# Four plain column tiles ahead of the seven-product sets in the first feed-forward, with the norm product, the first loads and the odd pool moved

## The chip, the cores and the metric

The kernel runs on one core of one Trainium2 chip. The metric is the device time of one execution in microseconds; the runs of the kernel before have a median of 1270.05 us (1269.68 to 1270.89, three runs). All names of lines (L463) are lines of the kernel before, unless a row comes from the changed kernel and says so.

## The reference

One block on x of shape 512 x 1024 in float32: a feed-forward with half weight, a mixer, a second feed-forward with half weight, and a final RMS norm.

```
x = x + 0.5 * swiglu(rmsnorm(x, g1), ffn1_w_gu, ffn1_w_down)     # D_FF = 2816
x = x + hybrid_mixer(rmsnorm(x, gm), w_in, ...)                  # conv + gated linear attention
x = x + 0.5 * swiglu(rmsnorm(x, g2), ffn2_w_gu, ffn2_w_down)
return rmsnorm(x, final_g)

swiglu(h, w_gu, w_down): g, u = split(h @ w_gu);  (silu(g) * u) @ w_down
```

The gate and the up half of `w_gu` are 2816 columns wide each, which is 22 column tiles of 128, and the reduction over 1024 is 8 k tiles.

## The kernel before

**Precision and weights.** x lies transposed in SBUF, 8 tiles `x[k]` of 128 features by 512 positions. Every float32 operand is split into a high and a low part (`wh`/`wl` for weights, `opA`, `opB` or `tp` pairs for data), and each product is three matmuls: wh by high, wh by low, wl by high. Weights arrive by DMA on SP's queue into `f` tiles (L248); ScalarE casts the high part (L273) and VectorE subtracts it for the low part (L274). `Weights.issue` does this, two units ahead of the matmuls, and `STEPS` holds the order of the units; the `f` ring has 10 tiles in the feed-forwards, `wh` and `wl` three each.

**First stage of a feed-forward.** `mm_group` (L325) multiplies the four column tiles 0 and 1 of gate and up, k by k, twelve matmuls of 512 columns for one k. Its data operands are x times the gain, not yet normed (`Norm.add`: L377 or L374 the high part, L378 the low part, L383/L386 the square, L387 the running sum `acc`). Behind the sixth k tile (`if k == 5`), `norm.finish` issues the product of `acc` with a matrix of ones (L407, L408) and the chain that makes 1/rms: transpose L410, small operations L411 to L434, copy L419, transpose L423. Its result `row` scales the group's results as they leave PSUM (L437).

**Sets.** The other 20 column tiles of each half go through ten sets of two tiles by a scheme of seven products in place of eight (m1, p2, q6, p5, q7, p4, p3). A product is 24 matmuls of 256 columns (L463), so a set has 168. The data operands of the products (`Operands.make`) are made once, from x normed with `row`: `normed` (L554, four instructions for a quarter), differences of quarters (L501 to L510), then a cast on ScalarE (L487) and a subtraction on VectorE (L488). A set's weights are four blocks of 512 KB; VectorE adds one sum (L261) and POOL's queue adds three by accumulating DMAs (L252). In the first feed-forward `xo.make("m1")` and `xo.make("p2")` come straight behind the group, then the two pairs of results are taken out of PSUM (times `row`, silu L568, product L437).

**The rest.** The down projection runs from `hid` (L301 to L303 with `opB` operands). The mixer's last three projections, w_out_conv, w_out_gla and w_o, have split `tp` tiles as data operands: 8, 8 and 4 column tiles by `mm_single` (L301 to L303, 24 matmuls each, 480 in all) and four by `mm_group` (L325, 96). The second feed-forward transposes X on TensorE in between (L645, L646).

**Order.** TensorE, VectorE, ScalarE and POOL run their streams in order, each in an order that the tile framework's scheduler chose from the program's text; SP's and POOL's queues issue DMAs in order too. At the start of the program the loop over k issues `x[k]`'s load and, for k of 0, 1, 2 and 4, `W.issue()`; the very first of these also loads the four blocks of the first set, because `loads` places a set's blocks six steps ahead of its first product.

**Places in SBUF.** Pools are stacked: `front`, `keep` (X), `wh`, `wl`, `opA`, `acc_row`, and then the pools of the phase. In the mixer these are `f` (4 tiles), the odd pool (`cpool`, small constants) and `tp` (50 tiles of 2048 bytes). In the built program of the kernel before, `opA` and `wh` tiles start 96 bytes behind a multiple of 2048, `opB` tiles 1120 bytes behind one, and the mixer's `tp` tiles 32 bytes behind one.

Of the kernel before, what the change touches and what calls it, by code (L numbers as in the profile page):

```python
# [15 lines left out]
P = 128  # L16
# [19 lines left out]
V_G1, V_GM, V_G2, V_GLA, V_CONV, V_GB = 0, 8, 16, 24, 32, 56  # L36
NVEC = 60
WARM = 10


def k_parts(kt):
# [53 lines left out]

PLAN = []
STEPS = []
ENDS = []  # L100
# [5 lines left out]
        PLAN.append(u)  # L106


def ffn_plan(up, down, slow):
    units(group(up, KD, (0, DFF, P, DFF + P), slow))  # L110
    firsts = []
    for s in range(1, KF // 2):
        firsts.append(len(PLAN))
        PLAN.extend((up, 4 * j, 4, (i * DFF + s * HW,), HW) for i in range(2) for j in range(2))
    STEPS.extend(order(firsts))
    units(full(down, KF))
    ENDS.append(len(STEPS))
# [23 lines left out]
    ENDS.append(len(STEPS))  # L141


ffn_plan("ffn1_w_gu", "ffn1_w_down", True)
mixer_plan()
ffn_plan("ffn2_w_gu", "ffn2_w_down", False)


def offset(n):
# [5 lines left out]
def block_kernel(ctx: ExitStack, tc: tile.TileContext, xT, vecs, gf, gup, wgl, wts, out):  # L155
# [236 lines left out]
    def rstd_rows(accs, width):  # L392


        n = len(accs)
        cnt[0] += 1
        i = cnt[0]

        def small(tag):
            t = acc_row.tile([P, HEADS * 16], F32, tag=tag, name=f"{tag}{i}")  # L400
            return t[:, : 16 * n]

        v, s, r, q = small("st_v"), small("st_s"), small("st_r"), small("st_q")
        for a, acc in enumerate(accs):
            h, l = split(acc)
            st = AUX()
            nc.tensor.matmul(st, ones_r, h, start=True, stop=False)  # L407
            nc.tensor.matmul(st, ones_r, l, start=False, stop=True)  # L408
            t = T()
            nc.vector.transpose(t, st)  # L410
            nc.vector.tensor_scalar(  # L411
                out=v[:, 16 * a : 16 * (a + 1)],
                in0=t.rearrange("p (b c) -> p b c", c=32)[:, :, 0],
                scalar1=1.0 / width, scalar2=EPS, op0=ALU.mult, op1=ALU.add)
        newton_rsqrt(r, v, s, q)
        rows = []
        for a in range(n):
            t = T()
            nc.vector.tensor_copy(  # L419
                t.rearrange("p (b c) -> p b c", c=32),  # L420
                r[:, 16 * a : 16 * (a + 1)].unsqueeze(2).to_broadcast([P, 16, 32]))
            row = acc_row.tile([P, S], F32, tag="row", name=f"row{i}") if n == 1 else T()
            nc.vector.transpose(row, t)  # L423
            rows.append(row)
        return rows
# [106 lines left out]
            sets[n].run(p)  # L532


    def ffn(up, down, norm, nxt):
        xh, xl = norm.h, norm.l
        rows = []

        def finish(k):
            if k == 5:  # L540
                rows.append(norm.finish())

        o = mm_group(up, KD, (0, DFF, P, DFF + P), xh, xl, extra=finish, slow=nxt is not None)
# [15 lines left out]
            return xn[j, l]  # L559

        xo = Operands(normed, 4)
        xo.make("m1")
        xo.make("p2")
        hid = [tile_of("hid", [P, 2, S])]
        for e in range(2):
            s, t = T(), T()
            mul(s, o[2 * e], row)
            nc.scalar.activation(s, s, AF.Silu)  # L568
            mul(t, o[2 * e + 1], row)
            mul(hid[0][:, e], s, t)  # L570

        def up_set(i):
            h = tile_of("hid", [P, 2, S])
# [74 lines left out]
    def last_down(us, split_hid):  # L648
# [72 lines left out]

        with tc.manual_schedule(engines={ENG.PE, ENG.DVE, ENG.Activation, ENG.Pool}):

            early = keep.tile([P, 1], F32, tag="early", name="early")
            nc.scalar.activation(early, hl[1][:, 1, 0:1].bitcast(F32), AF.Square)
            nc.scalar.activation(early, early, AF.Sqrt)
            for t in range(NTB):
                sm = keep.tile([P, 8], F32, tag="fin", name=f"fin{t}", bufs=2)
                fin.append([sm[:, i : i + 1] for i in range(6)])
                part(t, 0)  # L730
                if t > 0:
                    rstd(t - 1)
                    store(t - 1, 0)
                part(t, 1)
                if t > 0:
                    store(t - 1, 1)
            rstd(last)
            store(last, 1)
            store(last, 0)


    def mixer(norm, nxt):
# [16 lines left out]
        gl_raw = cpool.tile([P, KD, RANK], F32, tag="glraw", name="gl_raw")  # L759
        nc.sync.dma_start(gl_raw, wgl)  # L760
        gl_w = cpool.tile([P, KD, 3, 2 * RANK], F32R, tag="glw", name="gl_w")
        reset = T()
        nc.gpsimd.memset(reset, 1.0)
        nc.gpsimd.memset(reset.rearrange("p (c t) -> p c t", t=CH)[:, :, 0:1], 0.0)
# [299 lines left out]
    with phase("small1", **FFN):  # L1064
        W.phase(1)
        n1 = Norm(V_G1)
        for k in range(KD):
            nc.sync.dma_start(x[k], xT[k])
            if k < 2 or k % 2 == 0 and k < 6:
                W.issue()  # L1070
        W.early = 5
        for k in range(KD):
            n1.add(k, sooner=True)
        nm = Norm(V_GM)
        ffn("ffn1_w_gu", "ffn1_w_down", n1, nm)
    with phase("small2", f=4, small=1, tp=50):
        W.phase(2)
        n2 = Norm(V_G2)
        mixer(nm, n2)
    with phase("small3", **FFN):  # L1080
        W.phase(5)
        ffn("ffn2_w_gu", "ffn2_w_down", n2, None)


# [41 lines left out]
```

## Time and profile before

| | us |
|---|---|
| median of three runs | 1270.05 |
| the profiled execution | 1270.03 |
| its span (first to last instruction) | 1268.3 |
| TensorE busy in the span | 1231.4 |
| VectorE, ScalarE, POOL busy | 700.8, 502.4, 121.1 |
| mean granted TensorE clock | 0.987 of full speed |

What lies around the span is 1270.03 - 1268.3 = 1.7 us. A row of the timeline gives the start in us, the time to the end of its last instruction, engine, line, operation, output and inputs, the count, and in brackets the engine's idle time just before with what ended it. Matmuls overlap their neighbours, so the rate is read from the distance of starts, not from durations.

### The profile page before, as it was taken

What the parts mean: (1) busy time and instruction counts of PE and PEld (TensorE: products, weight loads), DVE (VectorE), ACT (ScalarE), POOL (GpSimd) and SP (SyncE); (2) the same over time, 40 slices, a digit from 0 to 9 for tenths busy, and PEclk for the clock granted to TensorE, in tenths of its full rate; (3) what the DMA queues carried; (4) which work ended last, traced back from release to release, by engine and by line L of the source; (5) the groups of instructions that cost most, each with busy time, mean ns of one, the idle gap of its engine ahead of it and who ended that gap; (6) DMA issues with size and microseconds to landing.
All of it is one profiled execution on the core that took longest, in us unless ns stands there. A gap on an engine that the chain in (4) does not pass through costs nothing.

```text
span 1268.3 us, 16985 instructions
## 1 busy us (share of the span) xinstructions
PE 1231.4 (97%) x7018; PEld 1081.6 (85%) x7018; DVE 700.8 (55%) x823; ACT 502.4 (40%) x640; POOL 121.1 (10%) x137
## 2 busy tenths in 40 slices
PE   8799999999999999999999999999889999999996
PEld 6699999988878788888888888888679999998885
DVE  6876666633365664453585334445676666663335
ACT  5454444522242542222334222323364444452233
POOL 1011111000010071000112000000011111100003
PEclk9799999999999999999999999999899999999999
DMA  8377777532013232222223333231558777763201
GB/s 299 84 181 195 182 182 187 173 115 67 36 53 120 87 97 83 67 84 83 83 83 100 100 100 90 94 100 34 189 131 198 185 187 175 187 181 98 67 1 67
DMA packets 43613, 152.91 MB, mean 121 GB/s; under 512 B 5040, under 2 KB 5168, under 8 KB 43536
## 3 DMA queue, kind: packets, MB, share of 16 engines
q1 hardware_dynamic: 34752, 120.34, 28.4%
q0 software_dynamic: 8640, 31.46, 14.1%
q8 instruction: 55, 0.90, 0.3%
q14 instruction: 22, 0.18, 0.0%
q10 hardware_dynamic: 144, 0.03, 0.0%
HBM read 118.26 MB, written 2.10 MB: 95 GB/s over the span
## 4 chain that ended last, share of the span: by engine, by line
PE 89%; DVE 4%; ACT 3%; issue 2%; DMA 2%; SPq 0%; POOL 0%; DVEq 0%; ACTq 0%
PE mm L463 29%; PE mm L302 13%; PE mm L301 13%; PE mm L303 13%; PE mm L325 5%; PE mm L662 2%; PE mm L661 2%; PE mm L660 2%; PE mm L343 1%; PE aux L302 1%; PE aux L303 1%; PE aux L301 1%; PE mm L344 1%; PE mm L342 1%; DVE wl L274 1%
## 5 line engine op out<-in xcount | busy, mean ns | idle before, releaser
L273 ACT CAST wh<-f 128x1024 fp32r<-128x1024 f32 (+1 forms) x281 | 293.5, 1046 | 614.7 <-PE mm L302 233.7
L274 DVE TENSOR_TENSOR wl<-f,wh 128x1024 fp32r<-128x1024 f32 (+1 forms) x281 | 344.8, 1229 | 269.1 <-ACT wh L273 267.1
L463 PE MATMUL mm<-opA,wh 128*128 128x256 f32 x1280 | 235.1, 284 | 3.5 <-ACT opA L487 2.8
L463 PEld LDWEIGHTS mm<-opA,wh 128*128 128x128 f32 x1280 | 200.8, 193 | 4.5 <-ACT opA L487 3.0
L463 PE MATMUL mm<-opB,wh 128*128 128x256 f32 x960 | 179.7, 287 | 7.7 <-ACT opB L487 6.7
L463 PE MATMUL mm<-opA,wl 128*128 128x256 f32 x640 | 181.8, 284 | 0.4 <-DVE wl L274 0.4
L301 PE MATMUL mm<-opA,wh 128*128 128x512 f32 x416 | 163.5, 393 | 0.0
L302 PE MATMUL mm<-opA,wh 128*128 128x512 f32 x416 | 162.9, 392 | 0.0
L303 PE MATMUL mm<-opA,wl 128*128 128x512 f32 x416 | 162.1, 390 | 0.0
L463 PEld LDWEIGHTS mm<-opB,wh 128*128 128x128 f32 x960 | 152.9, 195 | 9.0 <-ACT opB L487 7.6
L463 PE MATMUL mm<-opB,wl 128*128 128x256 f32 x480 | 137.3, 286 | 0.0
L463 PEld LDWEIGHTS mm<-opA,wl 128*128 128x128 f32 x640 | 123.3, 193 | 0.7 <-DVE wl L274 0.7
L252 POOL DMA_DIRECT2D f<-f x60 | 51.7, 861 | 628.4 <-DVE wl L274 294.6
L463 PEld LDWEIGHTS mm<-opB,wl 128*128 128x128 f32 x480 | 93.7, 195 | 0.0
L301 PEld LDWEIGHTS mm<-opA,wh 128*128 128x128 f32 x416 | 78.1, 188 | 16.4
L303 PEld LDWEIGHTS mm<-opA,wl 128*128 128x128 f32 x416 | 78.1, 188 | 16.1
L302 PEld LDWEIGHTS mm<-opA,wh 128*128 128x128 f32 x416 | 78.1, 188 | 16.1
L437 DVE TENSOR_TENSOR tp<-mm,tp 128x512 f32<-128x512 f32 x36 | 24.8, 691 | 105.8 <-PE mm L303 105.1
L303 PE MATMUL mm<-tp,wl 128*128 128x512 f32 x160 | 63.0, 394 | 0.0
L301 PE MATMUL mm<-tp,wh 128*128 128x512 f32 x160 | 63.0, 394 | 0.0
L302 PE MATMUL mm<-tp,wh 128*128 128x512 f32 x160 | 63.0, 394 | 0.0
L325 PE MATMUL mm<-opA,wh 128*128 128x512 f32 x192 | 50.8, 409 | 4.7 <-ACT wh L273 4.7
(204 smaller groups left out, 1709.8 us busy)
## 6 DMA issues: line engine op xcount, KB each, us to landing
f<-wts SPq DMA_DIRECT2D x219, 512.0 KB, 3.7
f<-f POOLq DMA_DIRECT2D x60, 512.0 KB, 4.8
X<-xT SPq DMA_DIRECT2D x8, 256.0 KB, 6.7
y<-tp SPq DMA_DIRECT2D x8, 256.0 KB, 2.2
f<-wts SPq DMA_DIRECT2D x2, 256.0 KB, 5.0
bf<-gf SPq DMA_DIRECT2D x2, 256.0 KB, 4.4
tp<-gup SPq DMA_DIRECT2D x6, 32.0 KB, 1.8
gl_raw<-wgl SPq DMA_DIRECT2D x1, 64.0 KB, 1.7
```

Of the source, the lines that this page charges most:

```text
L252: nc.gpsimd.dma_start(out_, a, accum_op=ALU.add)
L273: nc.scalar.copy(h[:, :w], raw[:, :w])
L274: nc.vector.tensor_tensor(out=l[:, :w], in0=raw[:, :w], in1=h[:, :w].bitcast(F32), op=ALU.subtract)
L301: nc.tensor.matmul(o, wh, ah, start=first, stop=False)
L302: nc.tensor.matmul(o, wh, al, start=False, stop=False)
L303: nc.tensor.matmul(o, wl, ah, start=False, stop=last)
L325: nc.tensor.matmul(o[c], w[:, s : s + P], a[k], start=k == 0 and j == 0, stop=k == kt - 1 and j == 2)
L437: (eng or nc.vector).tensor_tensor(out=out_, in0=a, in1=b, op=ALU.mult)
L463: nc.tensor.matmul(to, ww[:, s], aa[:, t], start=fresh and k == 0 and e == 0 and j == 0, stop=k == 3 and j == 2, skip_group_check=True)
L660: nc.tensor.matmul(o[t][e], a, wh, start=k == 0, stop=False)
L661: nc.tensor.matmul(o[t][e], a, wl, start=False, stop=False)
L662: nc.tensor.matmul(o[t][e], b, wh, start=False, stop=k == KF - 1)
```

## The change

- In the first feed-forward (`plain = 4`) the column tiles 2 and 3 of gate and up are multiplied plainly too: four `mm_single` of 24 matmuls of 512 columns each stand between the group and the sets, and nine sets are left in place of ten. The operand of q6 is made behind the second of these pairs. The second feed-forward keeps `plain = 2`.
- The taking out of the first pair of results now stands between `make("m1")` and `make("p2")`, in both feed-forwards.
- The product with ones follows the third k tile in the mixer and the second feed-forward, and stays behind the sixth in the first.
- With plain units in the plan, the first set's blocks are loaded later; the loop over x issues `W.issue()` for k of 0, 1 and 3.
- The four small tiles of the norm chain move from `acc_row` to `front`, `early` and `fin` from `keep` to `front`, and the odd pool gets 272 unused columns. In the built program X then starts 1120 bytes later, `wh`, `wl`, `opA` and `acc` 1024 bytes later, the mixer's `tp` tiles 1088 bytes later (1120 bytes behind a multiple of 2048), and `f`, `opB`, `hid` and `bf` where they were.

```diff
+ODD_FILL = 272
+PLAIN1, PLAIN2 = 4, 2
-def ffn_plan(up, down, slow):
+def ffn_plan(up, down, plain, slow):
     units(group(up, KD, (0, DFF, P, DFF + P), slow))
+    for f in range(2, plain):
+        units(single(up, KD, f * P))
+        units(single(up, KD, DFF + f * P))
     firsts = []
-    for s in range(1, KF // 2):
+    for s in range(plain // 2, KF // 2):
...
-            t = acc_row.tile([P, HEADS * 16], F32, tag=tag, name=f"{tag}{i}")
+            t = front.tile([P, HEADS * 16], F32, tag=tag, name=f"{tag}{i}")
...
-    def ffn(up, down, norm, nxt):
+    def ffn(up, down, norm, nxt, plain, at):
...
-            if k == 5:
+            if k == at:
                 rows.append(norm.finish())
...
         xo = Operands(normed, 4)
+        hid = []
+        def plain_pair(f, g, u):
+            if f % 2 == 0:
+                hid.append(tile_of("hid", [P, 2, S]))
+            s, t = T(), T()
+            mul(s, g, row)
+            nc.scalar.activation(s, s, AF.Silu)
+            mul(t, u, row)
+            mul(hid[-1][:, f % 2], s, t)
         xo.make("m1")
+        plain_pair(0, o[0], o[1])
         xo.make("p2")
-        hid = [tile_of("hid", [P, 2, S])]
-        for e in range(2):
-            s, t = T(), T()
-            mul(s, o[2 * e], row)
-            nc.scalar.activation(s, s, AF.Silu)
-            mul(t, o[2 * e + 1], row)
-            mul(hid[0][:, e], s, t)
+        plain_pair(1, o[2], o[3])
+        for f in range(2, plain):
+            g = mm_single(up, KD, f * P, xh, xl)
+            u = mm_single(up, KD, DFF + f * P, xh, xl)
+            if f == 3:
+                xo.make("q6")
+            plain_pair(f, g, u)
...
-            early = keep.tile([P, 1], F32, tag="early", name="early")
+            early = front.tile([P, 1], F32, tag="early", name="early")
...
-                sm = keep.tile([P, 8], F32, tag="fin", name=f"fin{t}", bufs=2)
+                sm = front.tile([P, 8], F32, tag="fin", name=f"fin{t}", bufs=2)
...
+        cpool.tile([P, ODD_FILL], F32, tag="fill", name="odd_fill")
...
         def gate_k(k):
-            if k == 5:
+            if k == 2:
                 rows.append(norm.finish())
...
             nc.sync.dma_start(x[k], xT[k])
-            if k < 2 or k % 2 == 0 and k < 6:
+            if k < 2 or k == 3:
                 W.issue()
...
-        ffn("ffn1_w_gu", "ffn1_w_down", n1, nm)
+        ffn("ffn1_w_gu", "ffn1_w_down", n1, nm, PLAIN1, 5)
...
-        ffn("ffn2_w_gu", "ffn2_w_down", n2, None)
+        ffn("ffn2_w_gu", "ffn2_w_down", n2, None, PLAIN2, 2)
```

How the change moves instructions shows at three places. In the rows a name such as `f_121` is one tile of the pool `f`.

The first is SP's queue at the start of the program, before:

```order
L248 DMA f_121<-wts 128x512
L1068 DMA X<-xT 128x512
L248 DMA f_124<-wts 128x1024
L248 DMA f_126<-wts 128x1024
L248 DMA f_128<-wts 128x1024
L248 DMA f_130<-wts 128x1024
L1068 DMA X<-xT 128x512
L248 DMA f_138<-wts 128x512
L1068 DMA X<-xT 128x512
L248 DMA f_145<-wts 128x1024
```

and now (L254 is the weight load, L1087 the load of x):

```order
L254 DMA f_121<-wts 128x512
L1087 DMA X<-xT 128x512 x2
L254 DMA f_129<-wts 128x512
L1087 DMA X<-xT 128x512 x2
L254 DMA f_137<-wts 128x1024
L1087 DMA X<-xT 128x512 x4
L254 DMA f_210<-wts 128x1024
L254 DMA f_212<-wts 128x1024
```

The four blocks of the first set (f_124 to f_130) stood ahead of the second x tile; now all of x stands ahead of them, and five plain units too.

The second is VectorE in the first feed-forward, from the moment `row` is there, before:

```order
L423 STREAM_TRANSPOSE row_329<-tp_327 128x512
L554 SCALAR_TENSOR_TENSOR hid_360<-X,vec,row_329 128x256 x4
L554 SCALAR_TENSOR_TENSOR hid_369<-X,vec,row_329 128x256 x3
L488 TENSOR_TENSOR opB_366<-hid_360,opB_365 128x1024
L554 SCALAR_TENSOR_TENSOR hid_369<-X,vec,row_329 128x256
L437 TENSOR_TENSOR tp_379<-mm_211,row_329 128x512
L437 TENSOR_TENSOR tp_380<-mm_212,row_329 128x512
L488 TENSOR_TENSOR opB_375<-hid_369,opB_374 128x1024
```

and now (L280 weights' low part, L443 taking results out, L494 an operand's low part, L560 a normed quarter):

```order
L429 STREAM_TRANSPOSE row_325<-tp_323 128x512
L280 TENSOR_TENSOR wl_390<-f_218,wh_389 128x1024
L560 SCALAR_TENSOR_TENSOR hid_357<-X,vec,row_325 128x256 x4
L443 TENSOR_TENSOR tp_367<-mm_194,row_325 128x512
L443 TENSOR_TENSOR tp_368<-mm_195,row_325 128x512
L494 TENSOR_TENSOR opB_363<-hid_357,opB_362 128x1024
L443 TENSOR_TENSOR tp_382<-mm_196,row_325 128x512
L443 TENSOR_TENSOR hid_366<-tp_367,tp_368 128x512
L560 SCALAR_TENSOR_TENSOR hid_373<-X,vec,row_325 128x256 x4
L443 TENSOR_TENSOR tp_383<-mm_197,row_325 128x512
L280 TENSOR_TENSOR wl_428<-f_245,wh_427 128x1024
L494 TENSOR_TENSOR opB_379<-hid_373,opB_378 128x1024
```

The operands of m1 (opB_363) and of p2 (opB_379) are made later behind `row` than before, with results and plain weights between them.

The third is VectorE in the second feed-forward, where no plain pair stands ahead of the sets. Before, behind `row`:

```order
L554 SCALAR_TENSOR_TENSOR hid_7252<-X,vec,row_7212 128x256 x3
L488 TENSOR_TENSOR opB_7249<-hid_7243,opB_7248 128x1024
L554 SCALAR_TENSOR_TENSOR hid_7252<-X,vec,row_7212 128x256
L488 TENSOR_TENSOR opB_7258<-hid_7252,opB_7257 128x1024
L261 TENSOR_TENSOR f_7085<-f_7077,f_7081 128x1024
L274 TENSOR_TENSOR wl_7162<-f_7077,wh_7161 128x1024
L261 TENSOR_TENSOR f_7130<-f_7122,f_7126 128x1024
L274 TENSOR_TENSOR wl_7215<-f_7079,wh_7214 128x1024
L437 TENSOR_TENSOR tp_7262<-mm_7073,row_7212 128x512
```

and now, from the results of the group on:

```order
L443 TENSOR_TENSOR tp_7162<-mm_6982,row_7080 128x512
L443 TENSOR_TENSOR tp_7163<-mm_6983,row_7080 128x512
L443 TENSOR_TENSOR tp_7177<-mm_6984,row_7080 128x512
L443 TENSOR_TENSOR tp_7178<-mm_6985,row_7080 128x512
L280 TENSOR_TENSOR wl_7215<-f_6986,wh_7214 128x1024
L443 TENSOR_TENSOR hid_7161<-tp_7162,tp_7163 128x512
L560 SCALAR_TENSOR_TENSOR hid_7168<-X,vec,row_7080 128x256 x4
L443 TENSOR_TENSOR hid_7161<-tp_7177,tp_7178 128x512
L560 SCALAR_TENSOR_TENSOR hid_7194<-X,vec,row_7080 128x256 x2
L494 TENSOR_TENSOR opB_7174<-hid_7168,opB_7173 128x1024
```

The quarter that p2 needs (hid_7252 before, hid_7168 now) stood ahead of the taking out of the group's results; now it stands behind it, behind the low part of q6's weights (wl_7215) and behind a product that waits for silu.

More of the change, by code (lines that the diff above doesn't have):

```diff
@@ L141, in mixer_plan @@
     ENDS.append(len(STEPS))
-ffn_plan("ffn1_w_gu", "ffn1_w_down", True)
+ffn_plan("ffn1_w_gu", "ffn1_w_down", PLAIN1, True)
 mixer_plan()
-ffn_plan("ffn2_w_gu", "ffn2_w_down", False)
+ffn_plan("ffn2_w_gu", "ffn2_w_down", PLAIN2, False)
 def offset(n):
```

## The prediction

> **What bounds the kernel now.** I read the busy times first, then TensorE's waits, then stretches of time around them.
>
> ```profile
> PE 1231.4 (97%) x7018; PEld 1081.6 (85%) x7018; DVE 700.8 (55%) x823; ACT 502.4 (40%) x640; POOL 121.1 (10%) x137
> ```
>
> ```profile
> engine line waited for: us in total, times, longest us
> PE mm L463 <- ACT opB L487: 6.7, 3, 3.1
> PE mm L325 <- ACT wh L273: 4.7, 2, 4.4
> PE aux L407 <- ACT tp L350: 3.6, 1, 3.6
> PE aux L645 <- ACT X L646: 3.4, 2, 2.6
> ```
>
> TensorE is the bound; a gain is either one of these waits, with the slow clock that follows it, or a shorter distance between matmuls. The stretches (length, busy time of each engine with instructions, granted clock, DMA share, GB/s) put the waits in two places, the start of the first feed-forward's sets and the start of the second's:
>
> ```profile
> core 0: us, PE busy (x) PEld busy (x) DVE busy (x) ACT busy (x) POOL busy (x), PEclk, DMA share, GB/s
> 34.50:57.50 23.00, 13.82 (x69) 12.78 (x69) 21.21 (x32) 10.98 (x13) 0.00 (x0) 0.70 0.27 69
> 924.60:940.50 15.90, 10.91 (x76) 10.10 (x76) 13.08 (x21) 12.02 (x18) 0.85 (x1) 0.89 0.51 125
> ```
>
> In the first, VectorE is busy 21.2 of 23.0 us while TensorE does 69 matmuls: the operands of the products are the bound there. TensorE's timeline of the start and of that stretch:
>
> ```profile
> 7.84 1.07 PE L325 MATMUL mm<-opA,wl 128*128 128x512 f32 x4
> 13.34 3.58 PE L325 MATMUL mm<-opA,wh 128*128 128x512 f32 x8 [4.43 <-ACT wh L273]
> 17.67 1.98 PE L325 MATMUL mm<-opA,wh 128*128 128x512 f32 x8
> 20.39 1.98 PE L325 MATMUL mm<-opA,wh 128*128 128x512 f32 x8
> 33.58 1.07 PE L325 MATMUL mm<-opA,wl 128*128 128x512 f32 x4
> 39.15 0.63 PE L463 MATMUL mm<-opB,wh 128*128 128x256 f32 x2
> 39.79 0.63 PE L463 MATMUL mm<-opB,wh 128*128 128x256 f32 x2
> 52.68 0.58 PE L463 MATMUL mm<-opB,wh 128*128 128x256 f32 x1 [3.07 <-ACT opB L487]
> 72.36 0.40 PE L463 MATMUL mm<-opB,wh 128*128 128x256 f32 x2
> 72.72 0.40 PE L463 MATMUL mm<-opA,wh 128*128 128x256 f32 x2
> ```
>
> One k of the group is 12 matmuls in 20.39 - 17.67 = 2.72 us, 0.2267 each. A set's matmul takes (72.72 - 72.36)/3 = 0.120 at full clock, and (39.79 - 39.15)/3 = 0.213 while the clock is half. The group ends at 33.58 + 4 x 0.227 = 34.5.
>
> **Plain tiles for a set.** A set is 168 x 0.120 = 20.2 us. Four `mm_single` are 96 matmuls with `opA` data. Their distance stands in the mixer's singles (41 steps from the first row to the second):
>
> ```profile
> 402.83 0.39 PE L302 MATMUL mm<-opA,wh 128*128 128x512 f32 x1
> 412.12 0.39 PE L301 MATMUL mm<-opA,wh 128*128 128x512 f32 x1
> 245.99 6.01 PE mm L463 x48
> ```
>
> 9.29/41 = 0.2266, so 21.8 us: the swap itself costs +1.6. The third row, from the chain that ended last, is the end of the tenth set: 252.0.
>
> **The start.** The gap at 8.9 waits in ScalarE's stream, where the weight's cast stands behind `x[1]`:
>
> ```profile
> 1.72 1.85 SPq L248 DMA_DIRECT2D f<-wts  x4
> 3.61 1.30 SPq L1068 DMA_DIRECT2D X<-xT  x1
> 11.54 0.72 ACT L377 ACTIVATE opA<-X,vec 128x512 fp32r<-128x512 f32 x1 [6.21 <-DMA X<-xT]
> 15.28 0.72 ACT L377 ACTIVATE opA<-X,vec 128x512 fp32r<-128x512 f32 x1
> 16.42 0.71 ACT L377 ACTIVATE opA<-X,vec 128x512 fp32r<-128x512 f32 x1
> GB/s 0 193 310 328 350 418 401 415 408 418 406 425 411 341 265 273 369 227 16 115 191 194 199 178 178 0 0 0 0 0 0 0 0 0 188 161 101 249 0 150
> ```
>
> The last row has 1.5 us a number: 0.75 MB by 4.5 us, 1.25 by 6. `x[1]` now ends at 0.79 MB of the queue and not at 2.9; with under 1 us from the last byte to the landing it is there at about 5.6. ScalarE then spends 16.42 - 15.28 = 1.14 on each x tile and about 1 on each large cast: k = 1 to 7 and four weight casts end at 16.1, and the cast that the group needs for its fifth k at 16.9 is that one. TensorE so goes on from 8.75 with seven more k at 2.72 and the product with ones (0.5): the group ends at 28.3, 6.2 earlier. Bounds: the margin is 0.8, so a load later by 2 us would cost 1.2; the gain cannot pass 6.2.
>
> **The operands of the sets.** Before, the product with ones at 28.6 led to `row` at 33.8; now the product comes at 22.4, and a sum L261 (1.2) stands in that chain, so `row` is there at 28.9. TensorE is on plain tiles from 28.3 to 50.0. VectorE's stream behind `row`, by durations of these rows:
>
> ```profile
> 33.10 0.71 DVE L423 STREAM_TRANSPOSE row<-tp 128x512 f32<-128x512 f32 x1
> 33.85 2.86 DVE L554 SCALAR_TENSOR_TENSOR hid<-X,vec,row 128x256 f32<-128x256 f32 x7
> 36.64 1.23 DVE L488 TENSOR_TENSOR opB<-hid,opB 128x1024 fp32r<-128x1024 f32 x1
> 38.18 1.28 DVE L437 TENSOR_TENSOR tp<-mm,row 128x512 f32<-128x512 f32 x2
> ```
>
> A normed quarter costs 4 x 0.41, an operation of 1024 columns 1.13 in a row of them, one of 512 columns 0.6. Added up in the new order, m1's operand is complete at 34.5, p2's at 40.2, q6's at 54.3 with its weights at 56.1, p5's at 57.2. TensorE wants them at 50.0, 52.9, 55.8 and 58.7, so only q6 is short, by 0.3, and q7 behind it by about as much; I allow 1.3 for such stalls, 0 to 4 as bounds since VectorE runs without a pause from 28.9 to 67. Hence the nine sets end at 28.3 + 21.8 + 9 x 20.2 + 1.3, and 0.6 for the wait that the end of the sets has now, that is 233.5 against 252.0: **-18.5** (-15 to -20).
>
> What hides the plain tiles' results (eight L437 products of 512 columns and silu) is the same stretch of TensorE; without that cover they would cost 5 us.
>
> **Data from the mixer's tp tiles.** A row of the last w_o tiles and one 95 steps later:
>
> ```profile
> 871.76 0.39 PE L301 MATMUL mm<-tp,wh 128*128 128x512 f32 x1
> 893.92 0.40 PE L303 MATMUL mm<-tp,wl 128*128 128x512 f32 x1
> ```
>
> 22.16/95 = 0.2333, with the clock at full, where `opA` data give 0.2266 in the same phase with the same kind of weight tile. What differs is the place: `tp` tiles of the mixer start 32 bytes behind a multiple of 128, `opA`, `opB` and `wh` tiles 96 bytes. The fill brings `tp` to 96 too. If the place is the cause, 576 matmuls gain 0.0067 each: **-3.8**. No trace here shows one tile at both places, so the bounds are -3.8 and 0, and I take -3.8, because the distance is the same for 16 projections' worth of matmuls at different times and other engines' work.
>
> The Trainium skill, page "TensorE: Matmul & The Clock Gate", section "Wait — 56ns, not 53.3ns?", gives a warm matmul a fixed cost of about 2.5 ns beyond N/2.4 GHz, 215.7 ns for 512 columns, whatever its operands' place. Neither 226.6 nor 233.3 agrees with it; by that rule the fill would bring nothing (the first rival).
>
> **The second feed-forward.** Here p2's operand loses its place ahead of the group's end, and no plain tile covers it. Rows of ScalarE, VectorE and TensorE there:
>
> ```profile
> 927.68 1.05 ACT L273 CAST wh<-f 128x1024 fp32r<-128x1024 f32 x1 [8.08 <-PE mm L463]
> 928.75 1.28 ACT L568 ACT_TABLE_LOAD   x1
> 930.05 1.15 ACT L568 ACTIVATE tp<-tp 128x512 f32<-128x512 f32 x2
> 932.52 1.07 ACT L646 COPY X<-aux 128x512 f32<-128x512 f32 x2
> 930.29 0.28 PE L463 MATMUL mm<-opB,wl 128*128 128x256 f32 x1
> 940.25 0.39 PE L463 MATMUL mm<-opB,wh 128*128 128x256 f32 x1 [1.62 <-ACT opB L487]
> ```
>
> Now: m1 ends at 927.5 as before. The cast of q6's weights (927.7, perhaps 0.6 later since its accumulating DMA starts later) and its low part (to 930.5), then the table load and silu (931.2), then L437 (931.9), then the four L554 (933.5): only then come p2's cast (934.6) and low part (936.2). What waits on TensorE behind p2 is everything. Its 24 matmuls take 2.9 to 5.1 (full or half clock), so they end by 941.1; the weight cast of q7 needs p2's buffer and stands in ScalarE's stream ahead of q6's cast: 942.2, two copies of X (1.0), q6's cast to 944.3. TensorE resumes there where before it resumed at 940.25: **+4.0**. Bounds: +2.5 if the clock is full and nothing slips, +7 if the products that follow start at half clock (24 matmuls x 0.093 = 2.2) and ScalarE slips once more.
>
> The Trainium skill, same page, section "What's actually happening", says that the clock is set by free-running windows of about 3.4 us. The trace agrees: matmuls behind the idle times at 46 to 53 ran at 0.213, those at 940.25 at 0.120.
>
> **The product with ones elsewhere.** In the second feed-forward the scheduler had it ahead of the group already (the wait of 3.6 at L407 in the table), and its place is unchanged: 0. In the mixer it moves about 22 matmuls ahead, 5 us, between matmuls that are there anyway; its operands are ready by then, and no wait of TensorE hangs on the mixer's `row` (its only waits up to 440 are 0.7 and 0.6 on weights): 0, bounds -0.7 and +0.5.
>
> **Sum.** -18.5 - 3.8 + 4.0 = -18.3 from the profiled execution's 1270.03 (span 1268.3, and 1.7 around it), which is the median 1270.05 within 0.02: **1251.7 us**.
>
> **Rivals.**
> - *The place is not the cause of 0.2333.* All else as above: 1251.7 + 3.8 = 1255.5. For it: the table of waits says nothing of places. Against: only those data tiles are slow.
> - *The second feed-forward does not pay.* If ScalarE's copies of X, which stood ahead of q6's cast (eight before, five to seven now), were the chain, p2 moves into time that was idle anyway: 1247.7. Against: VectorE's order above.
> - *The operands stay the bound of the first sets.* VectorE was busy 21.2 of 23.0 us there; if its stream behind `row` takes 25% longer (9 us more), half of it meets the plain tiles' slack and some 5 come out: 1256.7.
> - *Slower.* X, `wh`, `wl`, `opA` move too. If what counts is where weight tiles start, and the new place (1120 and not 96 behind a multiple of 2048) is the slow one, each of about 6,700 wide matmuls loses 0.0067: +44.7, and without the 3.8 the time is 1270.0 - 18.5 + 4.0 + 44.7 = 1300. It decides from (18.5 - 4.0)/0.0067 = 2,160 slowed matmuls. Against: `opB` data at 1120 and `opA` data at 96 go equally fast.
>
> **Chances.** The forecast's case 0.55, the first rival 0.26, the second 0.09, the third 0.06, slower 0.04. Half of the distance to each bound in the sum gives the forecast's own range, 1249 to 1256; a slip of the same 3.5 upon the first rival's 1255.5 gives 1259, and the second rival lies at 1247.7: the range is 1247 to 1259. A measurement of this kernel tells about 0.2% (2.5 us) from no change: faster by more 0.95, within 0.02, slower 0.03.
>
> **What will show it.** Right: the waits of L463 on L487 before 60 us nearly gone; TensorE without a gap from 5.6 to 230; first product of the sets at about 50; matmuls with `tp` data 0.2267 apart; a gap in the second feed-forward that starts at m1's end (not p2's) and about 4 us more from the group's end to q6. Wrong: `x[1]` landing after 8; VectorE behind TensorE at 50 to 67; `opA` matmuls at 0.233.

## The result and the profile after

The changed kernel takes **1250.53 us** in the median (1250.40 to 1250.63, four runs), beside 1270.47 (1269.68 to 1271.67) for the kernel before on the same chip: a ratio of 0.9842 with a 95% interval of 0.9825 to 0.9859, 19.9 us less. The forecast was 1251.7, with a range of 1247 to 1259. The profiled execution took 1250.56, its span is 1248.8; the spans differ by 1268.27 - 1248.83 = 19.44 us, and that is what the terms below are held against.

The busy times and the table of TensorE's waits of the changed kernel (us in total, times, longest); line numbers above 38 are 1 to 19 higher than before, the sets' products are L469 now, the singles L307 to L309, the group L331:

```profile
PE 1223.1 (98%) x6946; PEld 1075.9 (86%) x6946; DVE 695.9 (56%) x820; ACT 497.9 (40%) x634; POOL 125.3 (10%) x134
...
PE mm L469 <- ACT opB L493: 6.2, 2, 5.9
PE aux L413 <- ACT tp L356: 3.6, 1, 3.6
PE mm L469 <- ACT tp L474: 1.7, 2, 1.3
```

Of the waits of the kernel before, one row on operands at the start of the first feed-forward stands beside those shown ahead:

```profile
PE mm L463 <- ACT opA L487: 2.8, 1, 2.8
```

The waits for operands at the start of the first feed-forward (3.1 and 2.8 at the longest) and the 4.4 on a weight cast are gone. One wait of 5.9 on an operand is new, in the second feed-forward; the 3.6 at the mixer's end is the old one.

**The first feed-forward.** TensorE's timeline of the changed kernel: the first row of the group's second k, the last row of its eighth, the first row of the plain tiles, of the sets, of the down projection and of the mixer:

```profile
8.28 1.98 PE L331 MATMUL mm<-opA,wh 128*128 128x512 f32 x8
26.92 1.07 PE L331 MATMUL mm<-opA,wl 128*128 128x512 f32 x4
27.83 0.39 PE L307 MATMUL mm<-opA,wh 128*128 128x512 f32 x1
49.59 0.40 PE L469 MATMUL mm<-opB,wh 128*128 128x256 f32 x2
231.85 0.40 PE L307 MATMUL aux<-opB,wh 128*128 128x512 f32 x1
351.55 0.62 PE L331 MATMUL mm<-opA,wh 128*128 128x512 f32 x2
```

and of the kernel before, the last two of these:

```profile
251.84 0.40 PE L301 MATMUL aux<-opB,wh 128*128 128x512 f32 x1
371.55 1.07 PE L325 MATMUL mm<-opA,wh 128*128 128x512 f32 x4
```

The group ends at 27.8 (34.5 before), the sets start at 49.6, and the down projection starts 251.84 - 231.85 = 20.0 earlier. The mixer starts 20.0 earlier too, so nothing is given back in between. The stretch of plain tiles and the start of the sets, as before a row for each stretch (length, busy time of each engine with instructions, granted clock, DMA share, GB/s):

```profile
27.80:49.60 21.80, 21.80 (x98) 18.03 (x97) 21.23 (x34) 10.34 (x12) 1.73 (x2) 1.00 0.37 79
49.60:60.00 10.40, 10.40 (x88) 10.40 (x87) 10.14 (x12) 6.79 (x9) 0.86 (x1) 1.00 0.78 185
```

VectorE is as busy as it was (21.23 of 21.80, before 21.21 of 23.00), but TensorE is now busy without a gap beside it, at the full clock. VectorE's work is no longer what the sets wait for.

**Data from the tp tiles.** The last four w_o tiles, first and last row, 95 steps apart:

```profile
848.18 0.39 PE L307 MATMUL mm<-tp,wh 128*128 128x512 f32 x1
869.71 0.39 PE L309 MATMUL mm<-tp,wl 128*128 128x512 f32 x1
```

21.53/95 = 0.2266 where it was 0.2333. From the mixer's first matmul with tp data to its last the trace has 211.93 us, and 216.06 before: -4.1. From the mixer's start to the first of these it has 306.23 and 306.31.

**The second feed-forward.** TensorE from the mixer's end (869.7) on: the group's first row, the sets' first row, p2's first row, and the row at which TensorE comes back to q6 for good:

```profile
877.45 0.79 PE L331 MATMUL mm<-opA,wh 128*128 128x512 f32 x1 [0.27 <-ACT wh L279]
901.65 0.40 PE L469 MATMUL mm<-opB,wh 128*128 128x256 f32 x2
910.63 0.58 PE L469 MATMUL mm<-opB,wh 128*128 128x256 f32 x1 [5.95 <-ACT opB L493]
920.09 0.39 PE L469 MATMUL mm<-opB,wh 128*128 128x256 f32 x1 [0.29 <-ACT opB L493]
```

and before, where the mixer ended at 893.92:

```profile
901.68 0.80 PE L325 MATMUL mm<-opA,wh 128*128 128x512 f32 x1 [0.28 <-ACT wh L273]
924.66 0.40 PE L463 MATMUL mm<-opB,wh 128*128 128x256 f32 x2
```

| stretch of the second feed-forward | before | after | difference |
|---|---|---|---|
| mixer's last matmul to the group's first | 7.76 | 7.74 | 0.0 |
| group's first to the sets' first | 22.98 | 24.20 | +1.2 |
| sets' first to q6 for good (940.25 before) | 15.59 | 18.44 | +2.85 |
| q6 to the program's end | 328.0 | 328.7 | +0.7 |
| together | | | +4.8 |

So -20.0 - 0.1 - 4.1 + 4.8 = -19.4, the difference of the spans. The sum of the prediction was -18.3. About half a microsecond of the -20.0 is this profile's luck: in nine other profiles whose first feed-forward is the same the down projection starts at 231.90 to 232.52, in seven of them at 232.29 or later. Against the same 251.84 that is -19.3 to -19.9.

### The profile page after: what moved, and what is told of

It reads as the page before. It is cut to its first block, busy times and chain, and to the rows that moved or that the text cites. A ratio compares the mean times of both kernels' runs of the same rounds, so it can differ in the third digit from the quotient of the medians.

```text
span 1248.8 us, 16813 instructions
## 1 busy us (share of the span) xinstructions
PE 1223.1 (98%) x6946; PEld 1075.9 (86%) x6946; DVE 695.9 (56%) x820; ACT 497.9 (40%) x634; POOL 125.3 (10%) x134
## 5 line engine op out<-in xcount | busy, mean ns | idle before, releaser
L280 DVE TENSOR_TENSOR wl<-f,wh 128x1024 fp32r<-128x1024 f32 (+1 forms) x278 | 340.9, 1229 | 266.3 <-ACT wh L279 260.3
L469 PE MATMUL mm<-opA,wh 128*128 128x256 f32 x1216 | 222.1, 283 | 1.7 <-ACT tp L474 1.7
L469 PEld LDWEIGHTS mm<-opA,wh 128*128 128x128 f32 x1216 | 189.8, 192 | 2.3 <-ACT tp L474 2.1
L307 PE MATMUL mm<-opA,wh 128*128 128x512 f32 x448 | 175.9, 393 | 0.0
L469 PE MATMUL mm<-opB,wh 128*128 128x256 f32 x912 | 169.4, 286 | 6.2 <-ACT opB L493 6.2
L308 PE MATMUL mm<-opA,wh 128*128 128x512 f32 x448 | 175.2, 391 | 0.0
L309 PE MATMUL mm<-opA,wl 128*128 128x512 f32 x448 | 174.5, 390 | 0.0
L469 PE MATMUL mm<-opA,wl 128*128 128x256 f32 x608 | 172.1, 283 | 0.0
L469 PEld LDWEIGHTS mm<-opB,wh 128*128 128x128 f32 x912 | 144.3, 194 | 7.1 <-ACT opB L493 6.7
L469 PE MATMUL mm<-opB,wl 128*128 128x256 f32 x456 | 129.9, 285 | 0.0
L469 PEld LDWEIGHTS mm<-opA,wl 128*128 128x128 f32 x608 | 116.7, 192 | 0.0
L309 PEld LDWEIGHTS mm<-opA,wl 128*128 128x128 f32 x448 | 84.1, 188 | 17.3
L307 PEld LDWEIGHTS mm<-opA,wh 128*128 128x128 f32 x448 | 84.2, 188 | 17.2
L469 PEld LDWEIGHTS mm<-opB,wl 128*128 128x128 f32 x456 | 88.5, 194 | 0.0
L443 DVE TENSOR_TENSOR tp<-mm,tp 128x512 f32<-128x512 f32 x36 | 24.8, 691 | 102.5 <-PE mm L309 101.8
L307 PE MATMUL mm<-tp,wh 128*128 128x512 f32 x160 | 62.2, 389 | 0.0
L309 PE MATMUL mm<-tp,wl 128*128 128x512 f32 x160 | 62.2, 389 | 0.0
L678 PE MATMUL mm<-wh,opB 128*128 128x512 f32 x132 | 51.4, 389 | 0.0
```

The source lines that it names most:

```text
L280: nc.vector.tensor_tensor(out=l[:, :w], in0=raw[:, :w], in1=h[:, :w].bitcast(F32), op=ALU.subtract)
L307: nc.tensor.matmul(o, wh, ah, start=first, stop=False)
L308: nc.tensor.matmul(o, wh, al, start=False, stop=False)
L309: nc.tensor.matmul(o, wl, ah, start=False, stop=last)
L443: (eng or nc.vector).tensor_tensor(out=out_, in0=a, in1=b, op=ALU.mult)
L469: nc.tensor.matmul(to, ww[:, s], aa[:, t], start=fresh and k == 0 and e == 0 and j == 0, stop=k == 3 and j == 2, skip_group_check=True)
```

## The experiments

One is an edit of the kernel before, one the changed kernel once more; all others are edits of the changed kernel, so the time to compare with is 1250.5; the kernel before had medians of 1270.5 to 1271.0 beside them.

### Where tp tiles start: does the place make the distance?

The changed kernel without the fill (`cpool.tile([P, ODD_FILL], ...)` taken out):

```diff
-        cpool.tile([P, ODD_FILL], F32, tag="fill", name="odd_fill")
```

> The changed kernel without the 272 unused columns of the odd pool, so that the mixer's tp tiles start 32 bytes behind a multiple of 128 again and everything else stays. Theory (the place sets the distance): 576 matmuls with tp data stand 0.2333 apart again, +3.9 us, 1254.4. Rival (something else of the change, its order of instructions, made them 0.2267 apart): they stay at 0.2267 and the time at 1250.5.

The kernel before with nothing but 64 bytes put into the odd pool:

```diff
         gl_w = cpool.tile([P, KD, 3, 2 * RANK], F32R, tag="glw", name="gl_w")
+        cpool.tile([P, 16], F32, tag="fill", name="odd_fill")
```

> The kernel before with 16 unused columns (64 bytes) in the odd pool and nothing else: tp tiles start 96 bytes behind a multiple of 2048 and not 1120. Theory (the place within 128 bytes sets the distance): tp data 0.2267 apart, -3.9 us, 1266.4 beside 1270.3. Rival (it needs the larger shift, or the order of the changed kernel): 0.2333, 1270.3.

Measured: 1255.48 us without the fill (1252.50 to 1256.20), and 1266.84 for the kernel before with 64 bytes (1265.97 to 1267.94; ratio to the kernel before 0.9971, 0.9961 to 0.9981). First and last row of the last four w_o tiles, without the fill:

```profile
852.32 0.39 PE L307 MATMUL mm<-tp,wh 128*128 128x512 f32 x1
...
874.49 0.40 PE L309 MATMUL mm<-tp,wl 128*128 128x512 f32 x1
```

and of the kernel before with 64 bytes:

```profile
869.05 0.39 PE L301 MATMUL mm<-tp,wh 128*128 128x512 f32 x1
...
890.59 0.39 PE L303 MATMUL mm<-tp,wl 128*128 128x512 f32 x1
```

22.17/95 = 0.2333 and 21.54/95 = 0.2267. The same matmuls in the same order (in both pairs of traces every engine runs its instructions in the same order) take the one distance or the other when nothing but the place of their data moves, and 64 bytes are enough. The first rival (the place is not the cause) falls, and so does the alternative that the order of instructions did it.

### Is it the data's place, or the data's and the weights' together?

All pools 64 bytes earlier, so that weights and data alike start 32 bytes behind a multiple of 128:

```diff
-    fill = front.tile([P, 24], F32, tag="fill", name="fill")
+    fill = front.tile([P, 8], F32, tag="fill", name="fill")
```

> The changed kernel with all pools from ident on 64 bytes earlier: wh, wl, opA, opB and tp tiles all start 32 bytes behind a multiple of 128, instructions and order the same. Theory A (weight tile and data tile must start alike within 128 bytes): all matmuls stay at 0.2267 and 0.120, 1250.5 within 0.7. Theory B (data at 32 bytes are slow wherever the weights start): about 2,880 matmuls of 512 columns with opA and opB data and 576 with tp data at 0.2333, +23 us, 1274 or more if the products of 256 columns slow down too.

The same, and the odd pool 64 bytes larger, so that tp tiles alone stay at 96:

```diff
-ODD_FILL = 272
+ODD_FILL = 288
```

> The same 64 bytes earlier for wh, wl, opA and opB (32 bytes behind a multiple of 128), but the mixer's tp tiles at their place of the changed kernel (96 bytes). Theory A (alike within 128 bytes): only the 576 matmuls with tp data slow down to 0.2333, +3.9, 1254.4. Theory B (data at 32 are slow): tp data stay at 0.2267 and those with opA and opB data slow down, +19, 1270.

And the changed kernel with tp tiles at two other places (`ODD_FILL = 280` and `264`), with weights at 96:

> The changed kernel with 280 unused columns, so that tp tiles start at a multiple of 128, 32 bytes on from the weights' place (96) when places are counted within 128 bytes. Theory (only the difference of the two places counts; small products of tp data with the ones tile were 0.228 to 0.230 apart at a difference of 32 and 0.230 to 0.232 at 96): tp data 0.2285 apart, +1.1, 1251.6. Rival (any difference costs the full 0.0067): 0.2333, 1254.4; second rival (only a difference of 64 costs): 0.2267, 1250.5.

> The changed kernel with 264 unused columns: tp tiles start 64 bytes behind a multiple of 128, a difference of 96 to the weights' place. By the same small products: 0.2315 apart, +2.8, 1253.3. First rival 0.2333, 1254.4; second rival 0.2267, 1250.5.

First and last row of the last four w_o tiles, all at 32:

```profile
848.60 0.39 PE L307 MATMUL mm<-tp,wh 128*128 128x512 f32 x1
...
870.13 0.39 PE L309 MATMUL mm<-tp,wl 128*128 128x512 f32 x1
```

weights at 32 and tp at 96:

```profile
850.45 0.39 PE L307 MATMUL mm<-tp,wh 128*128 128x512 f32 x1
...
872.19 0.40 PE L309 MATMUL mm<-tp,wl 128*128 128x512 f32 x1
```

and weights at 96, tp at 0:

```profile
852.74 0.39 PE L307 MATMUL mm<-tp,wh 128*128 128x512 f32 x1
...
874.91 0.40 PE L309 MATMUL mm<-tp,wl 128*128 128x512 f32 x1
```

| weights start at (mod 128) | tp data at | distance, us | first tp matmul to last, us | time, us |
|---|---|---|---|---|
| 96 (changed kernel) | 96 | 0.2266 | 211.93 | 1250.53 |
| 32 | 32 | 0.2267 | 211.93 | 1251.64 (1249.45 to 1253.05) |
| 96 | 32 | 0.2333 | 216.07 | 1255.48 (1252.50 to 1256.20) |
| 96 | 0 | 0.2333 | 216.37 | 1256.19 (one run) |
| 96 | 64 | 0.2333 | 216.16 | 1253.82 (one run) |
| 32 | 96 | 0.2289 | 214.23 | 1253.60 (1252.08 to 1253.84) |

Data at 32 are not slow in themselves: with the weights at 32 as well, every distance stays (theory B's 1274 did not come; the median is 1.1 above the changed kernel's, where within 0.7 was expected, with its own runs 3.6 apart). What the fast rows share is that weight and data tiles start alike within 128 bytes; each pair that does not is slower. That the period is 128 bytes is not shown: no pair here differs by 128 or by 256, and a step's weights start 512 bytes behind those of the step before, so 256 or 512 fit as well. Two expectations were off. I had thought that the price grows with the difference (0.2285 at 0, 0.2315 at 64), from a few products with the tile of ones; it did not, all three other places cost 0.0067 with the weights at 96. And with the weights at 32 and the data at 96 the price was a third of that, 0.0022 and not 0.0067: the sign or the absolute place counts too, and why stays open. In that trace, whose starts are kept to the nanosecond, the three matmuls of a step of the last four tiles are not alike: 231.7 ns from wh by high to wh by low, 226.0 from there to wl by high, 229.0 from there to the next step. So 0.2289 is a mean of three distances, while in the rows with 0.2333 all three are 233 to 234. The single times of the kernels with data at 0 and at 64 lie 2.4 us apart though their tp stretches agree within 0.2; 1.9 of that is in the second feed-forward (below).

### Loads and plain tiles in the first feed-forward

Two plain tiles instead of four, all else as changed:

```diff
-PLAIN1, PLAIN2 = 4, 2
+PLAIN1, PLAIN2 = 2, 2
```

> The changed kernel with two plain column tiles in the first feed-forward: the load order, the places and the order of operands are the new ones, ten sets follow the group. Theory (VectorE's stream behind row bounds the start of the sets, and the plain tiles cover it): row comes some 5 us earlier than before and p2's operand 1.5 to 2 later behind it, so the sets end at about 249 and not 232.4, 1250.5 + 16.6 = 1267. Rival (the late x loads were the main loss, and the sets' stalls came from the loads of their blocks): the sets end at about 236, 1254.

Four loads that nobody reads between the first and the second x tile:

```diff
             if k < 2 or k == 3:
                 W.issue()
+            if k == 0:
+                for q in range(4):
+                    nc.sync.dma_start(tile_of("hid", [P, 1024]), <512 KB of wts>)
```

> The changed kernel with four more loads of 512 KB, whose data nobody reads, between the first and the second x tile on the loading queue, where the kernel before had the four blocks of the first set. Theory (the gap of 4.4 us at 8.9 and the half clock behind it hang on x[1]'s landing, and nothing later makes up for it): +6.2, 1256.7, with a wait of about 4.4 near 9 us. Rival (the plain tiles give slack that takes it up): within 1 us of 1250.5.

Measured: with two plain tiles **1273.42** (1271.97 to 1274.54), 22.9 more than the changed kernel and 2.4 more than the kernel before beside it (ratio 1.0017, 1.0007 to 1.0026). With the four loads 1255.55 (1255.44 to 1258.44), +5.0. With two plain tiles, two rows of TensorE's timeline, the sets' first product being the second of them, and the first row of the down projection:

```profile
13.43 3.78 PE L331 MATMUL mm<-opA,wh 128*128 128x512 f32 x8 [4.91 <-ACT wh L279]
...
43.30 0.58 PE L469 MATMUL mm<-opB,wh 128*128 128x256 f32 x1 [7.99 <-ACT opB L493]
...
256.55 0.40 PE L307 MATMUL aux<-opB,wh 128*128 128x512 f32 x1
```

and with the four loads:

```profile
13.14 3.62 PE L331 MATMUL mm<-opA,wh 128*128 128x512 f32 x8 [4.34 <-ACT wh L279]
...
238.35 0.40 PE L307 MATMUL aux<-opB,wh 128*128 128x512 f32 x1
```

The expectation for two plain tiles missed two things. The first is the loads: without plain units in the plan the first set's blocks stand six steps ahead of the set again, that is ahead of the second x tile, so the gap near 9 us came back (4.91 here). The load order is thus no separate part of the change: it follows from the plain units. The second is `row`, which was to come 5 us earlier than before and came at 40.5, 6.6 later. These are rows of ScalarE and VectorE with two plain tiles: a weight's cast and low part, the transposition that ends `row`, and the cast of m1's operand:

```profile
37.07 1.04 ACT L279 CAST wh<-f 128x1024 fp32r<-128x1024 f32 x1 [3.85 <-DMA f<-f]
38.15 1.22 DVE L280 TENSOR_TENSOR wl<-f,wh 128x1024 fp32r<-128x1024 f32 x1 [3.80 <-ACT wh L279]
39.75 0.71 DVE L429 STREAM_TRANSPOSE row<-tp 128x512 f32<-128x512 f32 x1
42.20 1.04 ACT L493 CAST opB<-hid 128x1024 fp32r<-128x1024 f32 x1 [4.08 <-DVE hid L560]
```

In VectorE's stream the low part of that weight stands ahead of the last two operations of the norm chain, and the cast before it waits for one of the first set's accumulating DMAs. m1's cast follows `row` by 1.7 here and by 1.7 in the kernel before (35.56 - 33.81). So the wait of 8.0 ahead of the sets is a late `row`, and not the new order of operands. That order shows at p2, whose cast starts 7.1 behind `row` (4.5 before), and TensorE waits 0.8 there. All together the sets end at 256.5, 4.7 later than before. This run therefore gives no price of the cover alone: its 22.9 hold the loads, the late `row` and the missing cover. The run with four plain tiles in the second feed-forward (below) is the cleaner one for that. The four loads measure the load order by itself: the down projection starts 238.35 - 231.85 = 6.5 later (5.8 against the latest of the ten profiles named above), where 6.2 was expected; the plain tiles took up none of it that this spread lets one see. (The time moved by 5.0 only, as the second feed-forward came out 1.6 shorter in that profile.)

### The operands of the second feed-forward

p2's operand straight behind m1's where no plain tile follows, measured twice, the second time beside the changed kernel on one chip:

```diff
         xo.make("m1")
+        if plain == 2:
+            xo.make("p2")
         plain_pair(0, o[0], o[1])
-        xo.make("p2")
+        if plain > 2:
+            xo.make("p2")
         plain_pair(1, o[2], o[3])
```

> The changed kernel with p2's operand made straight behind m1's in the second feed-forward, as in the kernel before; the first feed-forward keeps the new order. Theory (the taking out of the first pair between them delays p2 and so q6, measured +4.1 between the mixer's end and the program's end): 1246.5, the gap of 6 us at m1's end gone. Rival (the product with ones at the third k tile or the missing cover of X copies delays q6): the gap behind m1 goes, the same time is lost behind p2, 1250.5.

> The changed kernel itself once more, to stand beside the next run on the same chip: 1250.5, FFN2 from the mixer's end to the program's end 376 to 380 in the profiles so far.

> The changed kernel with m1's and p2's operands together in the second feed-forward, once more beside the changed kernel on one chip; every engine's order there is that of the kernel before. Theory (the late p2 operand costs some 3 of the 4 to 5 us, and the rest of the difference is where the slow-clock stretches fall): 2 to 3.5 below the changed kernel. Rival (the order costs nothing beyond 1 us, the earlier run's -1.3 was all of it): within 1 us of the changed kernel.

Measured: 1249.25 (1246.92 to 1249.54) the first time; the second time 1247.49 (1247.20 to 1250.94), beside 1250.41 (1248.81 to 1251.24) for the changed kernel. The intervals of the second time's ratios to the kernel before, 0.9828 (0.9814 to 0.9841) with the pair together and 0.9840 (0.9827 to 0.9853) for the changed kernel, overlap, so from the times alone the step is about -1.3 to -2.9, not the -4 that the theory gave. The stretches tell more. The group, and the stretch from the sets' start to q6, of the second run with the pair together:

```profile
878.10:901.20 23.10, 23.04 (x96) 19.04 (x97) 16.57 (x22) 7.07 (x8) 2.60 (x3) 0.94 0.61 189
901.20:916.70 15.50, 10.86 (x74) 9.96 (x73) 12.87 (x20) 11.95 (x18) 0.85 (x1) 0.89 0.54 125
```

of the changed kernel:

```profile
877.40:901.60 24.20, 24.15 (x96) 19.80 (x97) 13.90 (x17) 6.10 (x6) 2.61 (x3) 0.90 0.58 179
901.60:920.10 18.50, 11.71 (x72) 10.71 (x71) 15.64 (x26) 11.62 (x16) 0.85 (x1) 0.82 0.37 80
```

and of the kernel before:

```profile
901.70:924.70 23.00, 23.00 (x97) 18.95 (x98) 16.59 (x22) 6.99 (x7) 2.60 (x3) 0.95 0.62 189
924.70:940.20 15.50, 10.57 (x74) 9.79 (x72) 12.68 (x20) 11.87 (x17) 0.85 (x1) 0.89 0.51 124
```

From the sets' start to q6 there are 15.5 us with the operands together (15.0 in the first run), as in the kernel before, and 18.4 and 18.5 in the two profiles of the changed kernel. That is the price of the late operand: **2.9** in these profiles. Over all nine profiles with the late operand the stretch takes 17.5 to 18.7, over the four with both operands together (the two here, the kernel before and the same with 64 bytes) 15.0 to 15.6; the means lie 2.7 apart. The group ahead of it is another matter. Its 96 matmuls take 23.0 to 24.4 in these profiles by how much of them falls into the stretch at half clock behind the mixer's end (granted clock 0.95 and 0.90), and this does not go with the edit: the first run with the pair together had 24.4 at 0.89. Over all profiles here it ranged from 21.9 to 24.4. The third piece is near the end of the sets, where TensorE waits for a copy (L474) that stands behind a weight cast in ScalarE's stream: 1.2 to 2.0 in the profiles with nine sets in the first feed-forward and ten in the second (the changed kernel, with and without the pair), 0.3 to 0.4 in those with ten in both. The edit left it as it was, and with the longer group of the first run that is why the kernel with the pair together stays above the 1246.5 of the theory. The cast waits for an accumulating DMA: from its start on POOL's queue to the cast there are 4.8 us in the three profiles with ten sets in both (1124.99 to 1129.84 in the kernel before) and 5.7 to 6.5 in the ten profiles with nine and ten (1104.84 to 1110.66 in the changed kernel). Why the DMA takes longer there was not tried.

### Four plain tiles in the second feed-forward

```diff
-PLAIN1, PLAIN2 = 4, 2
+PLAIN1, PLAIN2 = 4, 4
```

> The changed kernel with four plain column tiles in the second feed-forward too. In the changed kernel TensorE loses some 11.7 us between 900 and 922 there. Theory (what covers the operands in the first feed-forward covers them here): that goes to about 1 and the swap of a set for 96 matmuls costs 1.6, so 1250.5 - 10.7 + 1.6 = 1241.4. Rival (the copies of X on ScalarE, which the second feed-forward has besides, keep the operands late): half of it stays, 1247; or nothing comes of it and the swap costs 1.6, 1252.

Measured: **1240.21** (1239.56 to 1240.45), ratio to the kernel before 0.9757 (0.9740 to 0.9775); the theory's 1241.4 is met. Waits, the plain tiles and the sets' start in its profile:

```profile
PE aux L413 <- ACT tp L356: 3.6, 1, 3.6
...
PE mm L469 <- ACT tp L474: 1.0, 2, 0.6
...
901.50:923.20 21.70, 21.70 (x97) 18.00 (x96) 20.53 (x31) 11.03 (x14) 2.58 (x3) 1.00 0.39 85
923.20:940.00 16.80, 16.80 (x141) 16.76 (x141) 15.95 (x17) 11.18 (x14) 0.85 (x1) 1.00 0.66 166
```

No wait for an operand of the sets is left, and TensorE is at the full clock in both stretches. The transposes and copies of X, which the rival put in the way, fit beside the plain tiles as well. This version beats both kernels, by 10.3 us and by 30.8 (its kernel before had 1271.0).

## Why the prediction was right, and where it was off

| step | predicted | measured in the profile |
|---|---|---|
| first feed-forward | -18.5 (-15 to -20) | -20.0 |
| data from tp tiles | -3.8 (-3.8 to 0) | -4.1 |
| second feed-forward | +4.0 (2.5 to 7) | +4.8 |
| product with ones elsewhere | 0 | -0.1 in the mixer |
| sum | -18.3 | -19.4 |

**The start.** The group was to end at 28.3 and ended at 27.8; the gap at 8.9 is gone. Four loads put back in its place cost 6.5, for a predicted 6.2: shown. The 0.5 by which the group ended early is no merit of the sum: it is the first k, which ended at 8.28 where 8.75 had been carried over from the profile before, and that end varies between profiles (8.28 to 8.98 in ten with the same first feed-forward).

**Plain tiles for a set.** The swap itself came as costed: 49.59 - 27.83 = 21.76 for the 96 matmuls. Two things make -20.0 of -18.5: the group's early end (0.5), and the allowance of 1.3 for stalls of q6 and q7, which was too large; with the 0.6 for the sets' end it was 1.9, and the nine sets took 0.8 more than 9 x 20.16. These are VectorE's rows of the changed kernel for `row`, m1's, p2's and q6's operands and q6's weights:

```profile
27.05 0.71 DVE L429 STREAM_TRANSPOSE row<-tp 128x512 f32<-128x512 f32 x1
32.18 1.23 DVE L494 TENSOR_TENSOR opB<-hid,opB 128x1024 fp32r<-128x1024 f32 x1
38.05 1.22 DVE L494 TENSOR_TENSOR opB<-hid,opB 128x1024 fp32r<-128x1024 f32 x1
51.63 1.22 DVE L494 TENSOR_TENSOR opB<-bf,opB 128x1024 fp32r<-128x1024 f32 x1
53.38 1.22 DVE L280 TENSOR_TENSOR wl<-f,wh 128x1024 fp32r<-128x1024 f32 x1
```

`row` was there at 27.8 and not 28.9, and the operands at 33.4, 39.3 and 52.9 for predicted 34.5, 40.2 and 54.3, q6's weights at 54.6 for 56.1. The chain's order was right and its forecast start 1.1 too late: the product with ones came at 21.9 and not 22.4 (the first k again), and from there to `row` the chain took 5.85 us, 0.6 more than before (5.25) and not the 1.2 of the sum L261 (L267 now). Of the 0.6 that the sum cost less, 0.3 lies in VectorE's wait for ScalarE's root, which the sum now fills, and 0.2 in a transposition that came sooner behind the product. So q6 was ready 0.8 ahead of TensorE (49.6 + 5.8 = 55.4) and not 0.3 behind. With that the third rival (the operands stay the bound) fell, though by a margin of less than 1 us.

**Data from tp tiles.** Right in size and in kind, on evidence that no row of the trace before could give: one tile seen at both places. The cause as the prediction put it, the place of the data, was half of it: what counts is the places of data and weights together. This also answers the fear behind the slower rival: moving `wh`, `wl` and `opA` together, by 1024 bytes or by 64, changes nothing (1251.64 with all at 32). The Trainium skill ("TensorE: Matmul & The Clock Gate", "Wait — 56ns, not 53.3ns?") gives a warm matmul a fixed cost and does not speak of places; read as it stands, it would have the fill bring nothing. The measured 0.2333 against 0.2266 for the same matmul speaks against that reading.

**The second feed-forward.** The sign and the mechanism were right: the gap stands at m1's end now, and p2's late operand makes q6 late. Its size was not: 2.85 (2.7 in the means above) and not 4.0. ScalarE's rows of the changed kernel, the cast of q6's weights and that of p2's operand:

```profile
904.21 1.05 ACT L279 CAST wh<-f 128x1024 fp32r<-128x1024 f32 x1 [7.60 <-DMA f<-f]
909.53 1.05 ACT L493 CAST opB<-hid 128x1024 fp32r<-128x1024 f32 x1 [0.40 <-DVE hid L560]
```

The step that failed is the start of that chain. I let the cast of q6's weights wait for m1's end and perhaps 0.6 more, 3.0 to 3.6 behind the sets' start; it waited for the DMA alone and came 2.6 behind (904.21 - 901.65). All that follows kept that lead: p2's cast ended 8.9 behind the sets' start for 9.9, q6 came back 18.4 behind for 19.6. That the sum came out close, +4.8, is luck: it has two pieces that the prediction did not have as terms, +1.2 of half clock in the group, which varies from run to run, and +0.7 behind q6, where the wait for L474 grew by 0.9 (1.3 and 0.4 in the two profiles). What the half clock costs there was in the bounds, but put behind the wait and not ahead of it. The second rival (the second feed-forward does not pay) fell: with p2's operand back in its place, q6 comes 2.9 earlier.

**The sum and the range.** The total is nearer to the forecast than its terms: the first feed-forward gained 1.5 more, and the second lost 0.8 more. The forecast's own range was added up loosely: half of the distances to the bounds, without that of the tp term, gives 1249.9 to 1255.2 and not 1249 to 1256.

**The product with ones.** Zero, as forecast: the mixer's stretch from its start to the first tp matmul is 306.23 for 306.31. It was not tried by itself.

## What to carry to other kernels

When an engine that prepares operands is the bound of a short stretch, it may not have to be made faster: in both feed-forwards here independent work of TensorE put ahead of that stretch covered it, and cost only its difference in matmul time (1.6 us, for 12 to 15 us of stalls and half clock); in the second it was the only edit, and paid 10 us. An order of instructions that is right under such cover can be wrong without it, as the pair of operands was here, so an edit that is shared by two places has to be costed at each. And where two groups of like matmuls differ in their distance by a few per cent, look at where their tiles start as well as for a wait.

## What the runs showed of the hardware that was not expected

- The distance of matmuls with 512 columns of this type was 0.2267 us when weight and data tile start alike within 128 bytes, and 0.2333 when they start 32, 64 or 96 bytes apart with the weights at 96; with the weights at 32 and the data at 96 it was 0.2289. Over 576 matmuls that is 2.3 to 4.4 us. Only these six pairs of places were tried, and the period of 128 bytes is not shown against 256 or 512.
- The same second feed-forward, with the same order on every engine, took 376.3 to 379.9 us from the mixer's end to the program's end in nine profiles: its group took 21.9 to 24.4 by how much of the half clock behind a wait of 3.6 us fell into it, and the wait for L474 took 0.3 to 2.0. A step of 2 us or less ahead of such a stretch cannot be read from one profile's total; the length of the stretch itself, 17.5 to 18.7 from the sets' start to q6, tells it better.
